# Hybrid HGRN2 and pooling block on one core: 8.25 products a half, pooled means in quarters, gates behind operands in the recurrent output projection

## The chip, the core and the metric

The kernel runs on one core of a Trainium2 chip, as one launch. Five engines with an instruction stream each take part: TensorE (PE), VectorE (DVE), ScalarE (ACT), GpSimd (POOL) and SyncE (SP), the last of which mainly issues DMA transfers; ScalarE and GpSimd issue a few too. The metric is the device time of a run in microseconds; the kernel before took 1466.38 us (median of 3 runs, 1464.82 to 1467.86).

## The reference

All tensors are float32, with 1024 tokens, width 1024, 8 heads of 128, and a hidden width of 4096. Cut to what matters:

```python
proj = x @ w_in                      # 7168 columns: q | f | i | og | pool_v | gate_a | gate_b
q = silu(q) * 128 ** -0.5
f = lb + (1 - lb) * sigmoid(f)       # lb from lb_logits, a softmax over two rows
# per head, in chunks: S_t = diag(f_t) S_{t-1} + (1 - f_t) i_t^T ;  o_t = S_t^T q_t
o = o * rsqrt(mean(o ** 2, per head) + 1e-6) * hgrn_norm_g * sigmoid(og)
a = o @ w_a
# trailing means over 2, 4, 8 and 16 tokens, one window to each quarter of the channels
b = per_group(mean_w(pool_v) - pool_v, w_pool) * pool_scale
mix = (sigmoid(gate_a) * a + sigmoid(gate_b) * b) @ w_out
x = LN(2 ** 0.25 * x + mix)
out = LN(2 ** 0.25 * x + relu(x @ w_up) ** 2 @ w_down)
```

## The kernel before

**Products.** Every large operand is split into a high part (a ScalarE cast to fp32r, L126 for weights and L131 for tokens) and a low part (a VectorE subtraction, L127 and L132). A product of two operands is three fp32r matmuls (high by high, high by low, low by high). The large products go by a two-by-two scheme with seven block products in place of eight: the 1024 tokens are two halves, the depth is two halves, and a `pair` takes two blocks of 128 weight columns. Its seven products are, with the operand on the weight side: `t0` for `p1`, `b_21` for `p2`, `t2` for `p6`, `t3` for `p7`, `t1` for `p5`, `t4` for `p4`, `b_22` for `p3` (with `twin` the middle four come as p7, p4, p6, p5). `t1` to `t4` are sums of weight blocks, made on VectorE in the tiles of the loaded blocks themselves (`make_t3` is L284). The token side has the operands `a11`, `a12`, `a22` and the sums `s1` to `s4`, resident in `xp`. One block product is `prod`: 12 matmuls of 128x128 by 128x512 into one PSUM bank (L212, L214, L215). Behind the products the quarters of the result are put together: `copied` (L275, ScalarE) empties a bank into a tile `c`, `added` (L279, VectorE) adds a second bank, and the function in `takes` does what the stage needs.

**Loads and rings.** Weight blocks of 512x128 (256 KB) come by SP's queue (`wide_block`, L223) into a ring of six tiles `raw`; `loaded_blocks` asks for blocks 11 and 21, one tile for the sum, then 12 and 22. Operand parts lie in a ring of ten tiles `w`. Results wait in a ring `c` of four plus two. A tile of a ring is given to its next use when the readers of its last use are done.

**Stages of the profiled execution.** To about 97 us: the value block `i` of the in-projection, with the tokens as the stationary side. `first_tokens` transposes x on TensorE (L170), `in_parts` splits it, `parts` splits rows of weights, `onto_chain` and `by_rows` multiply (`three`, from L501 on). In the source the calls of `parts(b11)` stand after `first_tokens("a11", ...)`; the ten short instructions for `lb`, `one_lb`, `e01` and `g_neg` (L440 to L449) stand ahead of both.

From 97 to 600 us: all other pairs of the in-projection up to gates 5, in the order of the list `ORDER`, and beside them the recurrence. The recurrence is a generator: `run` takes one turn of it after each block product (`next(turning[0], None)`). Half `n` is head n // 2, first or second 512 tokens. Its `prepare` pieces (VectorE, ScalarE, GpSimd), `turn_keys`, `scores`, `states`, `outputs` and `turn_outputs` are dealt over `PER_HALF` turns, in whole numbers by rounding a running sum (8.5: 8 and 9 alternating). The `inputs` pair of a head (q and f) must come before its half is prepared. `output_gates` and `gates` put sigmoids into DRAM (`og`, `ga`, `gb`). A `pooled` pair makes the trailing means in wide tiles `c` with a halo of 16 columns: `mean` works through two parts of 256 tokens with one to four additions each, and `put` stores the tile to `po`.

From 600 to 668.3 us: gates 6 and 7. Beside their 14 products goes the stream `pool_products`, by the counts of `POOL_AFTER` (how many of its steps follow each product), and what is left of the recurrence. A step multiplies a pooled operand by a block of `w_pool` (six matmuls, L113 to L115) and multiplies the result by a stored gate (`pb`). The weights of one group come by L618 into the single tile `tC`; their parts go round the four tiles `tD`, `tE`, `tF`, `og`. The tile `og` also holds the output gate of the half that is being finished (L1034), from which `put_output` stores the head, and with GpSimd's accumulating stores (L640) the sums `s1` to `s4` of the heads' outputs (`s` in the rows).

From 668.3 to some 780 us: the recurrent output projection `w_a` as four pairs with `turned` signs, the first two side by side. `o_operand` loads an operand of the heads' outputs (`o` in the rows, L618) and splits it, one name ahead of each product. `gated` loads a gate `ga` and a pooled result `pb`, multiplies (L1120) and adds; the first two pairs park their result. `room` is a ring of four tiles and `ga` one of twelve. Then come `w_out` and the first layer norm, the up projection with squared ReLU, and the down projection.

**Order.** From 97 to 668.3 us TensorE's order is the order of the program (`manual_schedule`). The order on the other engines, and on TensorE elsewhere, is chosen by the scheduler, by program order, `high_priority` and a model of times; `issue_after(i)` puts what is inside it behind instruction `i`. `behind_parts(name)` puts work behind the last two splits of a token operand.

The functions that the diff touches and those that call them:

Of the kernel before, what the change touches and what calls it, by code (L numbers as in the profile page):

```python
# [12 lines left out]
AF = mybir.ActivationFunctionType  # L13
# [16 lines left out]
PER_HALF = 8.5  # L30
# [21 lines left out]
def tile_hybrid_block(  # L52
# [105 lines left out]
    made_last, made_hi = {}, {}  # L158
# [108 lines left out]
    def pair(raw, rooms, takes, pz_tag="pj", twin=False, pc_tag="pj", turned=False):  # L267
# [35 lines left out]
        def t4():  # L303
            if twin:
                make_t2()
            if turned:
                minus_sum(b21, b11, b21)
            else:
                V.tensor_sub(b21, b21, b11)
            return w_part(b21)  # L310

        def t1():
            if turned:
                minus_sum(b12, b22, b11)
            else:
                V.tensor_sub(b12, b22, b11)
            return w_part(b12)
# [59 lines left out]
    turning = [iter(())]  # L377

    def run(*pairs, made=(), behind=()):

        for i, steps in enumerate(zip(*pairs)):
# [42 lines left out]
    with tc.tile_pool(name="xr", bufs=8, side="right", reuse_waits="tile") as xr:  # L424
# [15 lines left out]
        V.tensor_max(lb, prm[:, 0:8], prm[:, 8:16])  # L440
        V.tensor_sub(e01[:, 0:8], prm[:, 0:8], lb)
        V.tensor_sub(e01[:, 8:16], prm[:, 8:16], lb)
        A.activation(e01, e01, AF.Exp)
        V.tensor_add(lb, e01[:, 0:8], e01[:, 8:16])
        V.reciprocal(lb, lb)
        V.tensor_mul(lb, lb, e01[:, 0:8])
        V.tensor_scalar(one_lb, lb, -1.0, 1.0, ALU.mult, ALU.add)
        g_neg = e01[:, 0:8]
        V.tensor_scalar_mul(g_neg, g_col, -1.0)  # L449
# [109 lines left out]
        w = parts(b11)  # L559
# [60 lines left out]

    def o_operand(name):
# [23 lines left out]
    with tc.tile_pool(name="tmp", bufs=1, side="right", reuse_waits="tile") as tmp:  # L645
# [150 lines left out]
        def pooled(g):  # L796
# [3 lines left out]
            def mean(c, u):  # L800

                for lo in (QUARTER, 0):
                    pv = c[:, lo : lo + HALO + QUARTER]
                    cur = pv
                    for lev in range(g + 1):
                        s = 1 << lev
                        nx = small("pA" if lev % 2 == 0 else "pC", [P, HALO + QUARTER + HALO], 1)[:, : HALO + QUARTER]
# [722 lines left out]
```

## Time and profile before

| | before |
|---|---|
| median of 3 runs | 1466.38 us (1464.82 to 1467.86) |
| profiled execution, its time | 1466.59 us |
| its span | 1464.9 us |
| mean granted TensorE clock | 0.996 |
| DMA | 228.15 MB, mean 156 GB/s |
| L126 weight casts (ACT), 310 | 192.5 us |
| L127 weight splits (DVE), 310 | 212.1 us |
| L275 evictions (ACT), 96 | 55.8 us |
| L279 evictions (DVE), 95 | 64.8 us |

How the rows are read. A row of matmuls, casts or loads begins with its start in us from the start of the span and the mean duration of one; then engine, line, operation, out <- in, shapes and count; in brackets the idle time of the engine ahead of it and what ended that (`<-ACT c L275`: an instruction of ScalarE at line 275 that wrote a tile c). A row that begins with two times and a colon is a stretch of the span: its length, busy time of PE, of weight loads, DVE, ACT and POOL with counts, then the granted clock of TensorE, the mean share of the DMA engines in use, and GB/s. A row with `<-` between two instructions gives a kind of wait: total us, count, longest. SPq and POOLq are the sequencers that issue DMAs.

### The profile page before, as it was taken

Reading aid. Unit: us, or ns where it says so; the run is one execution under the profiler, and the core shown is the slowest. Engines: PE = TensorE matmul, PEld = TensorE weight load, DVE = VectorE, ACT = ScalarE, POOL = GpSimd, SP = SyncE. Lnnn points to the kernel's source line nnn. Section 1 sums busy time; section 2 is a strip of 40 time slices with the busy share of each in tenths; the row PEclk is TensorE's granted clock in tenths of the full one; section 3 lists DMA queues with packets and bytes.
Section 4 is the critical chain, followed back from the end, with each engine's and each line's share of the span. In section 5 each row is a group of like instructions: output and inputs, shape, how many; then the busy total and the mean of one; then the engine's idle time right before and its main releaser. Section 6 shows DMA issues by size and latency. Waiting matters only on the chain.

```text
span 1464.9 us, 20840 instructions
## 1 busy us (share of the span) xinstructions
PE 1435.5 (98%) x7377; PEld 1188.4 (81%) x7377; DVE 1100.1 (75%) x1807; ACT 759.0 (52%) x1383; POOL 107.6 (7%) x288
## 2 busy tenths in 40 slices
PE   8999999999999999999999999999999999999997
PEld 7788888788878888877788878888888888888886
DVE  4967886796797796477985598666666787777977
ACT  5545566655755655555542366555556443333435
POOL 0002011211211210000002100000000100000000
PEclk9999999999999999999999999999999999999999
DMA  7142245345435546788673135444447774445422
GB/s 259 58 137 87 73 126 169 80 134 155 109 87 146 142 116 184 211 300 286 204 232 113 61 99 180 144 154 148 157 148 261 280 262 142 166 132 170 129 72 115
DMA packets 187161, 228.15 MB, mean 156 GB/s; under 512 B 12176, under 2 KB 110512, under 8 KB 187056
## 3 DMA queue, kind: packets, MB, share of 16 engines
q1 hardware_dynamic: 181088, 212.91, 43.9%
q0 software_dynamic: 5184, 11.54, 4.0%
q10 hardware_dynamic: 784, 2.38, 0.5%
q8 instruction: 58, 0.95, 0.3%
q14 instruction: 47, 0.39, 0.1%
HBM read 149.70 MB, written 77.07 MB: 155 GB/s over the span
## 4 chain that ended last, share of the span: by engine, by line
PE 87%; DVE 6%; DMA 4%; issue 1%; ACT 1%; SPq 0%; DVEq 0%; POOL 0%; ACTq 0%
PE ps_pj L212 15%; PE ps_pj L215 14%; PE ps_pj L214 14%; PE ps_pj L1412 4%; PE ps_pj L1413 4%; PE ps_pj L1411 4%; PE ps_pj L114 2%; PE ps_pj L113 2%; PE ps_pj L115 2%; PE ps_tr L1412 1%; PE ps_tr L1413 1%; PE ps_tr L1411 1%; PE ps_sc L215 1%; DVE w L127 1%; PE ps_hg L215 1%
## 5 line engine op out<-in xcount | busy, mean ns | idle before, releaser
L212 PE MATMUL ps_pj<-act,w 128*128 128x512 f32 x1068 | 420.2, 395 | 10.8 <-ACT c L275 3.3
L215 PE MATMUL ps_pj<-act,w 128*128 128x512 f32 x1068 | 415.7, 391 | 1.3 <-DVE w L127 1.3
L214 PE MATMUL ps_pj<-act,w 128*128 128x512 f32 x1068 | 415.0, 390 | 0.0
L126 ACT CAST w<-raw 128x512 fp32r<-128x512 f32 x310 | 192.5, 622 | 278.1 <-PE ps_pj L214 201.7
L127 DVE TENSOR_TENSOR w<-raw,w 128x512 fp32r<-128x512 f32 x310 | 212.1, 686 | 92.8 <-ACT w L126 87.6
L212 PEld LDWEIGHTS ps_pj<-act,w 128*128 128x128 f32 x1068 | 200.7, 188 | 56.9 <-ACT c L275 4.6
L215 PEld LDWEIGHTS ps_pj<-act,w 128*128 128x128 f32 x1068 | 200.8, 188 | 45.2 <-DVE w L127 2.6
L214 PEld LDWEIGHTS ps_pj<-act,w 128*128 128x128 f32 x1068 | 200.8, 188 | 40.8 <-DVE act L132 0.2
L1373 ACT CAST act<-act 128x1024 fp32r<-128x1024 f32 x66 | 66.9, 1050 | 109.0 <-issue 35.0
L279 DVE TENSOR_TENSOR c<-c,ps_pj 128x512 f32<-128x512 f32 x95 | 64.8, 682 | 39.1 <-PE ps_pj L215 35.6
L1374 DVE TENSOR_TENSOR act<-act,act 128x1024 fp32r<-128x1024 f32 x66 | 79.5, 1220 | 18.5 <-ACT act L1373 17.4
L1413 PE MATMUL ps_pj<-act,act 128*128 128x512 f32 x240 | 93.0, 389 | 0.0
L1412 PE MATMUL ps_pj<-act,act 128*128 128x512 f32 x240 | 93.0, 389 | 0.0
L1411 PE MATMUL ps_pj<-act,act 128*128 128x512 f32 x240 | 92.5, 389 | 0.0
L275 ACT COPY c<-ps_pj 128x512 f32<-128x512 f32 x96 | 55.8, 581 | 3.1 <-issue 1.8
L284 DVE TENSOR_TENSOR raw<-raw,raw 128x512 f32<-128x512 f32 x43 | 29.6, 690 | 33.2 <-DMA raw<-in_w_in_dram 28.8
L1411 PEld LDWEIGHTS ps_pj<-act,act 128*128 128x128 f32 x240 | 45.0, 188 | 9.4
L1412 PEld LDWEIGHTS ps_pj<-act,act 128*128 128x128 f32 x240 | 45.0, 188 | 9.4
L1413 PEld LDWEIGHTS ps_pj<-act,act 128*128 128x128 f32 x240 | 45.0, 188 | 9.3
L1282 ACT ACTIVATE c<-c 128x512 f32<-128x512 f32 x61 | 38.5, 632 | 1.7
L1281 ACT ACTIVATE c<-c 128x512 f32<-128x512 f32 x46 | 29.1, 632 | 15.0 <-DVE c L279 15.0
L1367 DVE TENSOR_TENSOR act<-act,ps_pj 128x512 f32<-128x512 f32 x45 | 30.1, 682 | 6.0 <-PE ps_pj L1413 5.7
(416 smaller groups left out, 2680.5 us busy)
## 6 DMA issues: line engine op xcount, KB each, us to landing
h<-c SPq DMA_DIRECT2D x106, 256.0 KB, 2.7
raw<-in_w_in_dram SPq DMA_DIRECT2D x100, 256.0 KB, 3.3
act<-h SPq DMA_DIRECT2D x78, 256.0 KB, 3.0
draw<-in_w_down_dram SPq DMA_DIRECT2D x16, 1024.0 KB, 7.6
raw<-in_w_up_dram SPq DMA_DIRECT2D x56, 256.0 KB, 2.8
hf<-h SPq DMA_DIRECT2D x34, 256.0 KB, 3.0
s<-og POOLq DMA_DIRECT2D x28, 256.0 KB, 6.1
v<-v SPq DMA_DIRECT2D x16, 256.0 KB, 3.3
```

The lines of the kernel that those rows point to most:

```text
L126: A.copy(hi, src)
L127: V.tensor_sub(lo, src, f(hi))
L212: PE.matmul(ps, wh[:, k], th, start=first and k == 0, stop=False, skip_group_check=True)
L214: PE.matmul(ps, wh[:, k], tl, start=False, stop=False, skip_group_check=True)
L215: PE.matmul(ps, wl[:, k], th, start=False, stop=k == CH - 1, skip_group_check=True)
L275: A.copy(t, ps)
L279: V.tensor_add(t, t, ps)
L1373: A.copy(hi, src)
L1374: V.tensor_sub(lo, src, f(hi))
L1411: PE.matmul(ps, hh[:, w], wh, start=fresh and n == 0, stop=False, skip_group_check=True)
L1412: PE.matmul(ps, hh[:, w], wl, start=False, stop=False, skip_group_check=True)
L1413: PE.matmul(ps, hl[:, w], wh, start=False, stop=n == M - 1, skip_group_check=True)
```

## The change

Five edits. `PER_HALF` is 8.25 (8, 8, 8, 9 turns by rounding), inputs 7 precede gates 2, and the pool stream's steps beside gates 6 move towards the end by one product. In `pair`, `t2` is written into the tile of block 12 and `t1` into the tile of the difference, so block 11's tile is read last by `t2`. `mean` no longer works at once: it appends two entries to the list `later_on` (one for each part of 256 tokens, the second with the store), and `run` carries out one entry after each block product. At the start, weight rows 2 and 3 are split behind the token parts 1 and 3, and the lower-bound instructions behind all token parts. In `w_a`, the loads of `ga` and `pb` are put behind the last operand load issued, `room` has six tiles and serves all three results of a pair, and `ga` has ten.

```diff
-PER_HALF = 8.5
+PER_HALF = 8.25
@@ ORDER
-    ("gates", 2), ("inputs", 7), ("pooled", 3), ("gates", 3), ("gates", 4), ("gates", 5),
+    ("inputs", 7), ("gates", 2), ("pooled", 3), ("gates", 3), ("gates", 4), ("gates", 5),
-POOL_AFTER = {6: (1, 1, 1, 1, 1, 1, 2), 7: (2, 2, 2, 2, 0, 0, 0)}
+POOL_AFTER = {6: (0, 1, 1, 1, 1, 2, 2), 7: (2, 2, 2, 2, 0, 0, 0)}
@@ in_parts
-        made_last[name], made_hi[name] = (i.ins for i in split_into(xp[name][kp], src))
+        made_last[name], made_hi[name] = made_kp[name, kp] = [i.ins for i in split_into(xp[name][kp], src)]
@@ pair
-            return w_part(b11)
+            return w_part(b12)
         def make_t2():
             if turned:
-                minus_sum(b11, c["t"], b11)
+                minus_sum(b12, c["t"], b11)
             else:
-                V.tensor_add(b11, c["t"], b11)
+                V.tensor_add(b12, c["t"], b11)
         def t4():
...
-                V.tensor_sub(b21, b21, b11)
+                V.tensor_sub(b21, b21, b12)
         def t1():
...
-                V.tensor_sub(b12, b22, b11)
-            return w_part(b12)
+                V.tensor_sub(c["t"], b22, b12)
+            return w_part(c["t"])
@@ run
                     next(turning[0], None)
+                    if later_on:
+                        later_on.pop(0)()
@@ start: the ten lower-bound instructions leave L440 to L449
-        w = parts(b11)
+        w = parts(b11[:2])
+        for row, kp in zip(b11[2:], (1, 3)):
+            lo_done, hi_done = made_kp["a11", kp]
+            with tc.issue_after(lo_done), tc.issue_after(hi_done):
+                w += parts([row])
+        with behind_parts("a11"):
+            V.tensor_max(lb, prm[:, 0:8], prm[:, 8:16])
...
+            V.tensor_scalar_mul(g_neg, g_col, -1.0)
         first_tokens("a12", "tr")
@@ o_operand
-            split_into(xp[name][kp], loaded(src, c_tile))
+            t = c_tile()
+            last_load[0] = nc.sync.dma_start(out=t, in_=src).ins
+            split_into(xp[name][kp], t)
@@ pooled
-            def mean(c, u):
-                for lo in (QUARTER, 0):
-                    pv = c[:, lo : lo + HALO + QUARTER]
...
+            def mean(c, i, u):
+                later_on.append(lambda: quarter(c, u, QUARTER))
+                later_on.append(lambda: (quarter(c, u, 0), put(c, i, u)))
+            def quarter(c, u, lo):
+                pv = c[:, lo : lo + HALO + QUARTER]
...
             def first(c, i):
                 G.memset(c[:, :HALO], 0.0)
-                mean(c, 0)
-                put(c, i, 0)
+                mean(c, i, 0)
             def second(c, i):
-                mean(c, 1)
-                put(c, i, 1)
+                mean(c, i, 1)
@@ gated
             def take(src):
-                t = loaded(gad[j][u], mg_tile("ga", 12))
+                with tc.issue_after(last_load[0]):
+                    t = loaded(gad[j][u], mg_tile("ga", 10))
+                    more = loaded(pbd[j][u], mg_tile("gb", 2))
                 V.tensor_mul(t, t, src)
-                V.tensor_add(t, t, loaded(pbd[j][u], mg_tile("gb", 2)))
+                V.tensor_add(t, t, more)
@@ a_pair
-            room = mg_tile("room", 4)
+            room = mg_tile("room", 6)
-            return pair(raw, (c_tile, room, room), takes, "hg", True, turned=True)
+            return pair(raw, (room, room, room), takes, "hg", True, turned=True)
```

More of the change, by code (lines that the diff above doesn't have):

```diff
@@ L306, in t4 @@
             if turned:
[L307 removed]
+                minus_sum(b21, b12, b21)
             else:
[L309 removed]
+                V.tensor_sub(b21, b21, b12)
             return w_part(b21)
@@ L798, in pooled @@
             j, win = 2 * g, WINDOWS[g]
-            def mean(c, u):
-                for lo in (QUARTER, 0):
-                    pv = c[:, lo : lo + HALO + QUARTER]
[L804 to L807, printed above, removed]
-                        V.tensor_add(nx[:, 2 * s - 1 :], cur[:, 2 * s - 1 :], cur[:, s - 1 : HALO + QUARTER - s])
-                        cur = nx
-                    n = HALO
-                    if u == 0 and lo == 0:
-                        n += win - 1
-                        V.tensor_mul(cur[:, HALO:n], cur[:, HALO:n], inv_n[:, : win - 1])
-                        V.tensor_sub(pv[:, HALO:n], cur[:, HALO:n], pv[:, HALO:n])
-                    V.scalar_tensor_tensor(pv[:, n:], cur[:, n:], 1.0 / win, pv[:, n:], ALU.mult, ALU.subtract)
+            def mean(c, i, u):
[3 more added lines that the diff above has]
+                pv = c[:, lo : lo + HALO + QUARTER]
+                cur = pv
+                for lev in range(g + 1):
+                    s = 1 << lev
+                    nx = small("pA" if lev % 2 == 0 else "pC", [P, HALO + QUARTER + HALO], 1)[:, : HALO + QUARTER]
+                    V.tensor_add(nx[:, 2 * s - 1 :], cur[:, 2 * s - 1 :], cur[:, s - 1 : HALO + QUARTER - s])
+                    cur = nx
+                n = HALO
+                if u == 0 and lo == 0:
+                    n += win - 1
+                    V.tensor_mul(cur[:, HALO:n], cur[:, HALO:n], inv_n[:, : win - 1])
+                    V.tensor_sub(pv[:, HALO:n], cur[:, HALO:n], pv[:, HALO:n])
+                V.scalar_tensor_tensor(pv[:, n:], cur[:, n:], 1.0 / win, pv[:, n:], ALU.mult, ALU.subtract)
             def put(c, i, u):
```

25 lines of the change are left out of this document (12 added, 13 removed).

## The prediction, on record before the changed kernel ran

> **What bounds the kernel now.** I read the page's totals first, then the matmul waits with their times, then the stretches around each wait.
>
> ```profile
> span 1464.9 us, 20840 instructions
> PE 1435.5 (98%) x7377; PEld 1188.4 (81%) x7377; DVE 1100.1 (75%) x1807; ACT 759.0 (52%) x1383; POOL 107.6 (7%) x288
> 12.38:97.50 85.12, 84.36 (x384) 69.08 (x385) 67.86 (x115) 41.79 (x74) 0.76 (x7) 0.98 0.39 132
> 97.50:600.00 502.50, 496.50 (x3210) 415.65 (x3209) 392.63 (x794) 300.04 (x662) 83.36 (x236) 1.00 0.45 126
> 600.00:668.30 68.30, 64.83 (x274) 51.71 (x273) 46.52 (x73) 33.88 (x60) 2.62 (x3) 0.98 0.86 278
> 668.30:725.00 56.70, 53.19 (x230) 42.40 (x229) 48.03 (x78) 29.87 (x54) 0.00 (x0) 1.00 0.72 236
> 725.00:1464.90 739.90, 729.17 (x3245) 602.79 (x3243) 542.02 (x741) 349.10 (x530) 18.77 (x14) 1.00 0.47 159
> ```
>
> TensorE bounds it nearly everywhere. The rows give each stretch's length, then busy time of PE, weight loads, DVE, ACT, POOL, then the granted clock, DMA share and GB/s. The change moves no matmul out of the kernel, so it can win only PE's idle time before about 725 us and time at a reduced clock: 0.8 + 6.0 + 3.5 + 3.5 us in the four middle rows, and some at the start. Behind 725 us PE idles 10.7 us, nearly all at the end of the down projection, which the change leaves alone. The profiled execution took 1466.59 us, 1.7 us above its span; the median of the runs shown is 1466.38, so the two agree within 0.02%. About 0.2%, 2.9 us, is what a measurement of this kernel can tell from no change.
>
> **1. The start.** Two rows of windows, the first matmuls, and ScalarE ahead of them:
>
> ```profile
> 12.00:14.00 2.00, 1.62 (x5) 1.34 (x6) 2.00 (x6) 2.00 (x5) 0.00 (x0) 0.77 1.06 400
> 14.00:16.00 2.00, 2.00 (x6) 1.54 (x6) 1.52 (x6) 2.00 (x5) 0.00 (x0) 0.50 1.04 384
> 16.00:18.00 2.00, 2.00 (x10) 1.60 (x9) 1.18 (x2) 0.77 (x2) 0.00 (x0) 0.87 1.06 388
> 9.27 0.66 PE L170 MATMUL ps_sc<-ident,x 128*128 128x128 f32 x4 [1.28 <-DMA x<-in_x_dram]
> 9.76 0.60 PE L170 MATMUL ps_hg<-ident,x 128*128 128x128 f32 x4
> 12.38 0.50 PE L501 MATMUL ps_pj<-w,act 128*128 128x512 f32 x1 [2.02 <-ACT act L131]
> 7.87 0.62 ACT L126 CAST w<-b 128x512 fp32r<-128x512 f32 x1 [1.82 <-DMA b<-in_w_in_dram]
> 10.60 1.14 ACT L126 CAST w<-b 128x512 fp32r<-128x512 f32 x2 [2.12 <-DMA b<-in_w_in_dram]
> 11.76 1.05 ACT L131 CAST act<-ps_tr 128x512 fp32r<-128x512 f32 x2
> ```
>
> The token casts (L131) stand behind the casts of weight rows 2 and 3, which arrive at 10.6 us, though the transposes of the first two token tiles were done when PE fell idle, at 9.27 - 1.28 = 7.99. The change puts rows 2 and 3, and the ten lower-bound instructions, behind the token parts. ScalarE is free at 8.49 us, so two token casts of 0.5 us each end by about 9.6, before the last transposes end at 10.36: the 2.02 us go. Rows 2 and 3 are late next: cast from about 11.2 us, split by VectorE by 14.5, and needed only when the 24 matmuls of the first two weight rows (12 each, 729.17/3245 = 0.22 us a matmul by the last stretch) have gone by: 10.4 + 24 x 0.22 = 15.7. The clock was granted at 0.77, 0.50 and 0.87 in the three windows, a loss of 0.46 + 1.00 + 0.26 = 1.7 us, right behind that idle time. With the gap gone I take the loss as gone too: -3.7 us. Lower bound of the gain 0 (VectorE absorbs it later, below), upper 3.7.
>
> The Trainium skill (TensorE: Matmul & The Clock Gate, "Part 1: The HAM clock gate") says an idle activity window halves the clock and a busy one of about 3.4 us restores it; the three rows agree in depth and length. It also says the window runs freely, so the cold stretch varies from run to run, which speaks against booking it; by that the start is worth 2.0 us and the forecast would stand 1.7 us higher.
>
> **2. The recurrence.** The five waits of 0.88, 1.62, 0.74, 1.47 and 1.29 us make the 6.0:
>
> ```profile
> 263.59 0.50 PE L212 MATMUL ps_pj<-act,w 128*128 128x512 f32 x1 [0.88 <-ACT c L275]
> 289.36 0.50 PE L212 MATMUL ps_pj<-act,w 128*128 128x512 f32 x1 [1.62 <-ACT c L275]
> 319.77 0.50 PE L212 MATMUL ps_pj<-act,w 128*128 128x512 f32 x1 [0.74 <-DVE f L279]
> 433.32 0.50 PE L212 MATMUL ps_pj<-act,w 128*128 128x512 f32 x1 [1.47 <-ACT f L275]
> 437.62 0.50 PE L212 MATMUL ps_pj<-act,w 128*128 128x512 f32 x1 [1.29 <-DVE f L279]
> 120.00:590.00 470.00, 464.00 (x3058) 388.47 (x3057) 376.78 (x770) 281.00 (x623) 83.36 (x236) 1.00 0.45 125
> 420.00:450.00 30.00, 27.24 (x184) 22.36 (x183) 26.44 (x59) 18.89 (x40) 6.66 (x16) 1.00 0.43 109
> 510.00:540.00 30.00, 30.00 (x205) 25.21 (x203) 28.65 (x64) 16.45 (x40) 4.39 (x12) 1.00 0.46 130
> DVE raw L284 <- DMA raw<-in_w_in_dram: 28.8, 16, 4.5
> SPq L223 <- DVE w L127: 127.7, 43, 9.7
> ```
>
> All five are late evictions: VectorE is at 376.78/470 = 24.0 of 30 us, and in crowded windows PE waits. At 8.25 products a half, 17 halves have 140.25 products instead of 144.5: the same VectorE work in 3.0% less room, at most 24.8 of 30. Against it, the pooled quarters come one behind each product: no instruction more, but a burst of up to four quarters is spread over four products, and its four stores land up to four products later; the tiles they hold are asked for again only by the second pair after, so no wait follows. Yet the fullest window, 510 to 540 (the widest pooled pair), lost nothing, so spreading is not where the six are.
>
> T2 written into b12 and T1 into the difference's tile leaves the count of instructions. The second load of a pair can start two products earlier. The fourth, for whose arrival L284 waited 28.8 us in all, still waits for the split (L127) of the sixth product's operand, and T1 is now made one product before it is used instead of four. So I book 0: the waits change places. Bounds: -6.0 if all go, +5 if the 3% adds two windows like 420:450 (2.76 each). Inputs 7 ahead of gates 2 moves seven products and their four loads without a new one: 0.
>
> **3. Pool products beside gates 6 and 7.**
>
> ```profile
> 608.97 0.74 DVE L1034 SCALAR_TENSOR_TENSOR og<-ps_tr,e,og 128x512 f32<-128x512 f32 x1
> 610.00 2.62 POOL L640 DMA_DIRECT2D s<-og  x3 [25.82 <-DVE og L1034]
> 620.52 0.69 DVE L127 TENSOR_TENSOR og<-tC,tF 128x512 fp32r<-128x512 f32 x1 [2.31 <-DMA s<-og]
> 622.30 0.67 SPq L618 DMA_DIRECT2D tC<-in_w_pool_dram  x1
> 627.71 0.62 ACT L126 CAST tD<-tC 128x512 fp32r<-128x512 f32 x1 [3.37 <-DMA tC<-in_w_pool_dram]
> 628.90 0.50 PE L212 MATMUL ps_pj<-act,w 128*128 128x512 f32 x1 [2.16 <-ACT w L126]
> 630.30 0.50 PE L215 MATMUL ps_pj<-act,w 128*128 128x512 f32 x1 [0.67 <-DVE w L127]
> 632.00:634.00 2.00, 2.00 (x6) 1.52 (x6) 0.11 (x1) 0.00 (x0) 0.00 (x0) 0.50 1.08 344
> ```
>
> One chain: the last head's gain (L1034), its accumulating stores, the low half of the pool weights into the same tile (2.31 us late), the load of the next pool weights behind it, ScalarE stuck 3.37 us on that load with the operand of gates 6's last product queued behind, PE idle 2.16 + 0.67, and then 3.4 us at half clock, 1.7 us. Together 4.5. The recurrence ends four products earlier; in the instruction order of the changed kernel the split into og precedes the fourth product's operand of gates 6 instead of the sixth's, while ScalarE's cast of the next pool weights keeps its place before the seventh. The 14 products of gates 6 and 7 fill the stretch of 68.3 us, 4.9 us each with what goes beside them, so the load has two products, 9.8 us, more, against 3.37 needed: -4.5. In return L1034 and that split now have products with fewer pool steps between them; the store took 620.52 - 609.71 = 10.8 us, and VectorE can wait 2.31 + 1.4 us (one pool step of six matmuls less, 6 x 0.22) with operands queued behind. Bounds 0 to 3.7; I take 1.5, nearer to the old wait, which cost PE nothing. Net -3.0.
>
> **4. w_a.**
>
> ```profile
> 677.39 5.89 SPq L618 DMA_DIRECT2D ga<-ga  x4
> 683.69 0.32 SPq L618 DMA_DIRECT2D c<-o  x1
> 688.59 1.14 ACT L131 CAST act<-c 128x512 fp32r<-128x512 f32 x2 [3.36 <-DMA c<-o]
> 689.26 0.49 PE L212 MATMUL ps_hg<-act,w 128*128 128x512 f32 x1 [2.13 <-ACT act L131]
> 699.71 0.50 PE L212 MATMUL ps_pj<-act,w 128*128 128x512 f32 x1 [0.99 <-ACT room L275]
> 656.49 1.68 SPq L223 DMA_DIRECT2D raw<-in_w_a_dram  x3
> ```
>
> SP's queue was held 5.9 us by four gate loads; the operand behind them (683.69) came late: 2.13 us. In the new order all 28 operand loads precede the first gate load, so that goes, and six rooms instead of four take the 0.99. What comes: the gate products (L1120) stand behind the last operand splits on VectorE, and eight gate loads, three weight blocks and four pooled loads follow in a row. 15 x 256 KB at 236 GB/s are 16.7 us for some 17 us of VectorE work; a wait of 0 to 3 us, I take 1.0. Two weight blocks now queue behind operands of s2 that wait for gates 7's fourth product: gates 7's last three products of 12 matmuls and the two pool steps beside its fourth end that stretch, so the fourth ends near 668.3 - 3 x 2.7 - 2.7 = 657.5; with the split behind it the blocks are issued near 660 instead of 656.5. The second pair uses them from 668.3 + 2.7 = 671, and a load took 688.59 - 683.69 = 4.9 us: covered, by some 6 us. Net -2.1.
>
> The Trainium skill (DMA: Bandwidth & Descriptors, "Issuing engines are not separate DMA queues") has all issuers share the same 16 DMA engines; the stretches of 0.86 and 0.72 DMA share agree. By it reordering makes no bandwidth, and this part would be worth 0, the total 2.1 us more.
>
> Nothing else in the up and down projections gains or loses: T2 and T1 are made on VectorE there too, at 542 of 740 us busy.
>
> **Sum.** -3.7 + 0 - 3.0 - 2.1 = -8.8: span 1456.1, time 1457.8 us.
>
> **Rivals.**
> - Only the start: parts 2 to 4 exchange one wait for another (28.8 us of L284 and 10.8 us of store speak for it). 1466.6 - 3.7 = 1462.9.
> - It doesn't do what it says: VectorE is 67.86 of 85.12 us busy behind the start, and absorbs the lead, while 3 and 4 exchange waits: 1466.6. Against: VectorE's backlog begins with a wait for the transposes, which move along.
> - Slower: VectorE becomes the bound of the recurrence. If every second of the 16 halves has a window like 420:450, that is 8 x 2.76 = 22.1 in place of 6.0, +16.1, net +7.3: 1473.9. It ends above 1469.5 from (8.8 + 6.0 + 2.9)/2.76 = 6.4 such windows on. For it: the 3%; against it: 28.65 of 30 cost nothing at 510.
>
> **Chances.** The sum 0.50, only the start 0.18, no effect 0.12, VectorE bound 0.20. Faster takes the first and two thirds of the second, 0.62; same a third of the second and most of the third, 0.16; slower 0.22. The first case's own range is 1451 to 1463 (6.0 more won in part 2; or 5 lost there). To leave out 2 in 10 the whole reaches from 1451 to 1470.
>
> **What would show it.** Part 1: no wait of 2 us before the first L501, clock 1.00 from 12 to 18 us. Part 2: PE idle about 6 us from 97 to 600. Part 3: no ScalarE wait on tC, no reduced clock near 630; a DVE wait on s<-og instead. Part 4: no c<-o wait on ScalarE beside ga loads. Wrong if PE idles over 9 us in the recurrence, or a new wait of over 2 us with a halved clock appears around w_a.

## The result, and the profile after

The changed kernel takes 1462.19 us (median of 20 runs, 1457.27 to 1466.81), the kernel before 1466.12 in as many: a ratio of 0.9972, 95% interval 0.9962 to 0.9983. That is 3.9 us faster by the medians and 4.1 by the ratio, where 8.6 were forecast. The direction was right, half the gain is missing. The profiled execution took 1464.25 us, 2.1 above the median, with a span of 1462.6. One execution of a run below, c_gate_late, took 2054.45 us at a mean granted clock of 0.654, and is in no ratio.

The changed kernel's totals and stretches, cut where its own stages begin (columns as before: length, then busy time of PE, weight loads, DVE, ACT, POOL, then clock, DMA share, GB/s):

```profile
span 1462.6 us, 20884 instructions
PE 1435.4 (98%) x7377; PEld 1190.3 (81%) x7377; DVE 1100.2 (75%) x1807; ACT 759.2 (52%) x1383; POOL 106.7 (7%) x288
12.38:92.98 80.60, 80.12 (x376) 66.02 (x375) 65.89 (x114) 40.03 (x72) 0.76 (x7) 1.00 0.42 144
92.98:603.31 510.33, 501.68 (x3218) 418.93 (x3216) 393.97 (x796) 302.71 (x664) 85.11 (x239) 0.99 0.45 125
603.31:672.65 69.34, 63.32 (x266) 50.35 (x264) 48.73 (x78) 36.69 (x67) 0.00 (x0) 0.98 0.87 291
672.65:729.50 56.85, 56.85 (x252) 47.10 (x251) 49.63 (x81) 27.82 (x50) 0.00 (x0) 1.00 0.66 219
729.50:1462.60 733.10, 723.45 (x3222) 598.76 (x3221) 537.39 (x732) 345.94 (x523) 18.78 (x14) 1.00 0.46 159
```

The kernel before, cut at the same two stages (recurrence, pool products):

```profile
97.50:600.89 503.39, 497.39 (x3214) 416.38 (x3212) 393.21 (x795) 300.91 (x663) 83.36 (x236) 1.00 0.45 126
600.89:668.17 67.28, 63.81 (x270) 50.84 (x268) 45.94 (x73) 32.91 (x58) 2.62 (x3) 0.97 0.86 278
```

Stage by stage: the value block ends 4.5 us earlier (97.50 to 92.98). The recurrence is 6.9 us longer: TensorE's idle time is up from 6.0 to 8.65 us, and behind two of its waits the clock is lower (0.51 on average from 505.5 to 509 us, 0.57 from 566.5 to 570.5), which loses 1.7 us each time. The pool products are 2.1 us longer, idle time from 3.5 to 6.0. From w_a to the end the rest is 6.8 us shorter (796.7 to 790.0): w_a's stretch has no idle time at all. The idle time of the rest fell by 4.6 us (3.5 + 10.7 to 9.65); what the other 2.2 us are is not known. The sum is -2.3, the difference of the spans.

TensorE's long waits in the changed kernel, with the start's first product on top and two windows of the start below:

```profile
10.05 0.48 PE L493 MATMUL ps_pj<-w,act 128*128 128x512 f32 x1
310.05 0.50 PE L212 MATMUL ps_pj<-act,w 128*128 128x512 f32 x1 [1.04 <-ACT f L275]
449.18 0.50 PE L212 MATMUL ps_pj<-act,w 128*128 128x512 f32 x1 [2.18 <-ACT c L275]
505.64 0.80 PE L212 MATMUL ps_pj<-act,w 128*128 128x512 f32 x1 [2.25 <-DVE c L279]
565.42 0.50 PE L212 MATMUL ps_pj<-act,w 128*128 128x512 f32 x1 [2.08 <-ACT c L275]
645.46 0.80 PE L212 MATMUL ps_pj<-act,w 128*128 128x512 f32 x1 [4.96 <-ACT w L126]
12.00:14.00 2.00, 2.00 (x10) 1.67 (x9) 1.32 (x4) 2.00 (x5) 0.00 (x0) 1.00 1.05 405
14.00:16.00 2.00, 2.00 (x10) 1.67 (x9) 0.82 (x3) 1.17 (x3) 0.00 (x0) 1.00 1.05 386
```

The start is as forecast: the first product at 10.05 instead of 12.38 us, no wait, full clock. The five short late evictions of before are gone; one of 1.04 us and three of over 2 us stand elsewhere. A wait of 4.96 us in gates 7 is new.

### The profile page after: what moved, and what is told of

Same layout as the page of the kernel before. It is cut to its first block, busy times and chain, and to the rows that moved or that the text cites. A ratio compares the mean times of both kernels' runs of the same rounds, so it can differ in the third digit from the quotient of the medians.

```text
span 1462.6 us, 20884 instructions
## 1 busy us (share of the span) xinstructions
PE 1435.4 (98%) x7377; PEld 1190.3 (81%) x7377; DVE 1100.2 (75%) x1807; ACT 759.2 (52%) x1383; POOL 106.7 (7%) x288
## 4 chain that ended last, share of the span: by engine, by line
PE 85%; DVE 7%; DMA 4%; issue 2%; ACT 1%; SPq 0%; DVEq 0%; POOL 0%; ACTq 0%; POOLq 0%
PE ps_pj L212 14%; PE ps_pj L215 14%; PE ps_pj L214 14%; PE ps_pj L1425 4%; PE ps_pj L1426 4%; PE ps_pj L1427 4%; PE ps_pj L114 2%; PE ps_pj L113 2%; PE ps_pj L115 2%; PE ps_tr L1425 1%; PE ps_tr L1426 1%; PE ps_tr L1427 1%; PE ps_hg L215 1%; PE ps_hg L214 1%; PE ps_sc L215 1%
## 5 line engine op out<-in xcount | busy, mean ns | idle before, releaser
L215 PE MATMUL ps_pj<-act,w 128*128 128x512 f32 x1068 | 417.1, 391 | 0.6 <-DVE w L127 0.4
L126 ACT CAST w<-raw 128x512 fp32r<-128x512 f32 x311 | 192.9, 622 | 273.9 <-PE ps_pj L214 186.1
L127 DVE TENSOR_TENSOR w<-raw,w 128x512 fp32r<-128x512 f32 x311 | 213.0, 687 | 103.1 <-ACT w L126 101.8
L215 PEld LDWEIGHTS ps_pj<-act,w 128*128 128x128 f32 x1068 | 201.6, 189 | 44.6 <-DVE w L127 1.7
L284 DVE TENSOR_TENSOR raw<-raw,raw 128x512 f32<-128x512 f32 x43 | 29.6, 689 | 31.3 <-DMA raw<-in_w_in_dram 29.2
```

Source lines behind the costliest of these rows:

```text
L126: A.copy(hi, src)
L127: V.tensor_sub(lo, src, f(hi))
L215: PE.matmul(ps, wl[:, k], th, start=False, stop=k == CH - 1, skip_group_check=True)
```

## Experiments

All times are medians beside runs of the kernel before on the same chip; the ratio is to those. "c" stands for the changed kernel with the old counts: 8.5 products a half, the old order and the old pool counts. Line numbers are those of each run's own kernel: in the changed one the loads of L618 are L625, the accumulating stores of L640 are L651 and the gain of L1034 is L1046; in the runs with w_a's first operand late, L126, L127 and L215 are L128, L129 and L217, and L793 is L799.

| run | edit | us | ratio (95%) |
|---|---|---|---|
| after | the change | 1462.2 | 0.9972 (0.9962, 0.9983) |
| b_start | before + start | 1461.5 | 0.9970 (0.9960, 0.9981) |
| b_wa | before + w_a | 1460.0 | 0.9967 (0.9954, 0.9979) |
| b_both | before + start + w_a | 1457.4 | 0.9941 (0.9927, 0.9954) |
| a_old_count | c itself | 1453.8 | 0.9921 (0.9909, 0.9934) |
| c_new_order | c, inputs 7 first | 1455.5 | 0.9933 (0.9920, 0.9946) |
| c_mean_at_once | c, means at once | 1457.2 | 0.9931 (0.9915, 0.9946) |
| c_old_tiles | c, old operand tiles | 1457.0 | 0.9940 (0.9927, 0.9953) |
| a_old_pool | after, old pool counts | 1464.4 | 0.9991 (0.9978, 1.0003) |
| a_gate_late | after, gate load later | 1462.1 | 0.9969 (0.9958, 0.9980) |
| c_gate_late | c, gate load later | 1455.3 | 0.9926 (0.9912, 0.9939) |
| a_far_pool | after, one product on GpSimd | 1466.4 | 0.9998 (0.9987, 1.0009) |
| a_no_means | after, no means | 1452.3 | 0.9906 (0.9892, 0.9919) |
| a_no_accum | after, no accumulating stores | 1453.8 | 0.9913 (0.9901, 0.9926) |
| a_a11_late | after, w_a's first operand late | 1462.0 | 0.9969 (0.9956, 0.9982) |
| c_a11_late | c, w_a's first operand late | 1452.0 | 0.9903 (0.9888, 0.9918) |
| c_v_a11 | c_a11_late, pool weights not in og | 1466.0 | 0.9998 (0.9988, 1.0008) |
| c_np_a11 | c_a11_late, new pool counts | 1451.2 | 0.9882 (0.9866, 0.9899) |
| c_sp_a11 | c_a11_late, spread counts | 1452.2 | 0.9894 (0.9879, 0.9909) |

**Which part gains and which costs.** The start's hunks alone, w_a's hunks alone (`o_operand`, `gated`, `a_pair`), and both, on the kernel before:

> The kernel before with the start's edit alone (rows 2 and 3 behind token parts, lower-bound instructions behind all parts). Theory 1: the first product of inputs 0 begins 4 to 4.5 us earlier and nothing later gives it back: 4 us faster, 1462. Rival: VectorE or the loads of the stages behind absorb the lead: within 1 us of the kernel before.

> The kernel before with w_a's edit alone (loads of ga and pb behind the last operand load, six rooms). Theory 1: the waits of 2.13, 0.99, 0.29 and 0.25 us in w_a go, and no new one comes: 3.5 to 4.5 us faster, 1462. Rival: the DMA engines bound w_a, the order of the loads makes no difference: within 1 us. Forecast on record: 2.1 us faster.

> The kernel before with the start's and w_a's edits alone, old operand tiles, pooled means at once. If the parts add (start 4.2, w_a 5.6 less what the profile's spread makes): 1456 to 1458. The new operand tiles and the quarters, which the run with the old count has besides (1453.8), are then worth 2 to 4 us; the rival is that they are worth nothing: 1453 to 1455.

The start with its clock (first row, of b_start), and w_a (second row, of b_wa):

```profile
0.00:97.00 97.00, 93.80 (x442) 78.30 (x443) 71.46 (x123) 47.31 (x82) 2.82 (x35) 1.00 0.47 161
```

```profile
668.00:760.00 92.00, 91.59 (x404) 75.55 (x403) 76.97 (x124) 43.63 (x78) 0.00 (x0) 1.00 0.66 213
```

0.30% and 0.33% faster alone, 0.59% together: the two parts add, and make more than the whole change does (0.28%). So another part must cost. The count was undone, with all the rest left as changed:

```diff
-PER_HALF = 8.25
+PER_HALF = 8.5
-    ("inputs", 7), ("gates", 2), ("pooled", 3),
+    ("gates", 2), ("inputs", 7), ("pooled", 3),
-POOL_AFTER = {6: (0, 1, 1, 1, 1, 2, 2),
+POOL_AFTER = {6: (1, 1, 1, 1, 1, 1, 2),
```

> The changed kernel with 8.5 products a half, the old order (gates 2 before inputs 7) and the old pool counts. Start, operand tiles of a pair, quarters and w_a stay as changed. Theory 1: the 3% less room in the recurrence costs what the profile shows, some 6.5 us more excess between 97 and 600 us (three waits of 2.1 to 2.3 us with a lower clock behind two of them): without it about 1456 to 1458, and TensorE's idle time from 97 to 600 us at 6 us or less. Rival: quarters or the new operand tiles crowd VectorE, not the count: 1461 to 1464, idle time there stays over 8 us.

1453.8 us: 8.4 less than the changed kernel, 7.5 by the ratios. The three lines together cost that much; more than the forecast's sum of all gains is there without them. In the profiles all of it lies in the recurrence, cut as above where it and gates 6 begin: 500.57 us here, 510.33 as changed, while the pool products are no shorter (70.31 and 69.34). This is no accident of one execution: the other runs with 8.25 that leave VectorE's work and the stores alone (a_old_pool, a_gate_late, a_a11_late) have 510.5 to 510.8 us there, all runs with 8.5 on the changed kernel 500.4 to 502.7. Then one part of it, or one further part of the change, was put back or taken out. `c_new_order` has the first and third line of that diff alone, `a_old_pool` the third alone; `c_mean_at_once` calls both parts and `put` from `mean`; `c_old_tiles` has `pair` as before.

> 8.5 products a half and the old pool counts, but inputs 7 ahead of gates 2; all other edits as changed. Theory 1 (the count costs, since eight turns a half leave no turn without VectorE work): the order of the two pairs is innocent, 1453 to 1456, idle time of TensorE from 97 to 600 us within 2 us of the run with the old count. Rival (the swap crowds the stretch from 440 to 510 us, where two of the three long waits of the changed kernel lie): 1457 to 1460, with waits of about 2 us there.

> 8.5 products a half, old order and old pool counts; start, operand tiles and w_a as changed, but a pooled tile's two parts made at once and not one behind each product. Theory 1: quarters are worth at most 1 to 2 us (the waits at 433 and 437 us of the kernel before lie behind pooled 2 and went with them): 1454 to 1456. Rival: quarters carry the gain in the recurrence: 1457 or more.

> 8.5 products a half, old order and old pool counts; start, quarters and w_a as changed, but t2 written into block 11's tile and t1 into block 12's as before. Theory 1: the new tiles are worth 1 to 2 us in the recurrence, since the second load of a pair starts two products earlier (the waits of the split sum for a weight load fell from 28.8 to 23.9 us): 1454 to 1456. Forecast on record: nothing, 1454. Rival: they carry most of it: 1457 or more.

> The changed kernel with the old counts of pool steps, (1,1,1,1,1,1,2) beside gates 6. Theory 1: the new wait of 4.96 us in gates 7 comes from six products in a row with two pool steps each, which the four tiles f cannot serve (loads of gates and stores of results queue on SP, and the operand loads of w_a behind them). With one product fewer at two steps it shrinks to under 1.5 us and the lower clock behind it goes: about 5 us under the changed kernel, near 1457. Rival: the wait is there because the cast of a w_a operand stands ahead of a gate operand's cast on ScalarE, whatever the counts: 1461 to 1463, and a wait of 4 to 5 us remains in gates 7. Second rival: the old wait on the tile og comes back (2.2 us near the end of gates 6): 1459.

The order of the two pairs costs little, if anything: 0.12% by the ratios (1.8 us) with intervals that overlap by half, and the recurrence takes 502.53 us with it. Quarters and tiles are worth some 1.5 and 2.8 us by the ratios, both together 2.9 (b_both against a_old_count), with intervals that overlap; neither is settled as to its size. With old tiles a wait of the kernel before (437.62) is back in its place:

```profile
432.39 0.50 PE L212 MATMUL ps_pj<-act,w 128*128 128x512 f32 x1 [1.28 <-DVE f L279]
```

The pool counts are not the cost either: with the old ones at 8.25 the kernel is no faster (0.9991 against 0.9972, intervals that overlap a little). That leaves the 8.25, and c_new_order and a_old_pool differ in nothing else: 0.9933 against 0.9991, 8.5 us, with intervals far apart, and 502.53 against 510.80 us in the recurrence. In its pool stage a_old_pool shows the split into og waiting for the last head's stores, then SP's queue held by a gate load with a weight block behind it, and TensorE idle:

```profile
610.94 0.69 DVE L127 TENSOR_TENSOR og<-tC,tF 128x512 fp32r<-128x512 f32 x1 [5.46 <-DMA s<-og]
627.11 0.32 SPq L625 DMA_DIRECT2D f<-gb  x1
627.49 0.43 SPq L223 DMA_DIRECT2D raw<-in_w_in_dram  x1
633.30 0.49 PE L212 MATMUL ps_pj<-act,w 128*128 128x512 f32 x1 [2.79 <-DVE raw L301]
```

**Why the recurrence loses.** Of the changed kernel, how the wait at 505 us comes about: GpSimd issues three accumulating stores, SP a weight block; the DMA engines' share of that stretch and the packets of the two kinds of queue from 480 to 498 us (packets, MB, share of 16 engines); VectorE from the late block to the eviction that TensorE waits for; the clock behind it.

```profile
483.51 2.66 POOL L651 DMA_DIRECT2D s<-og  x3 [6.15 <-DVE og L1046]
484.10 0.38 SPq L223 DMA_DIRECT2D raw<-in_w_in_dram  x1
484.00:492.50 8.50, 8.50 (x40) 6.99 (x39) 1.86 (x5) 1.73 (x3) 2.29 (x4) 1.00 1.02 209
q0 software_dynamic: 432, 0.79, 30.4%
q1 hardware_dynamic: 1550, 1.34, 24.0%
493.91 0.69 DVE L284 TENSOR_TENSOR raw<-raw,raw 128x512 f32<-128x512 f32 x1 [6.90 <-DMA raw<-in_w_in_dram]
499.47 1.27 DVE L900 TENSOR_TENSOR_SCAN tA<-starts,f 128x256 f32<-128x256 f32 x2
504.91 0.67 DVE L279 TENSOR_TENSOR c<-c,ps_pj 128x512 f32<-128x512 f32 x1
504.00:506.00 2.00, 0.36 (x1) 0.36 (x2) 2.00 (x6) 1.98 (x7) 0.42 (x3) 0.88 0.38 129
506.00:508.00 2.00, 2.00 (x6) 1.52 (x6) 2.00 (x5) 1.99 (x4) 0.00 (x0) 0.50 0.01 2
508.00:510.00 2.00, 2.00 (x8) 1.62 (x7) 1.97 (x4) 0.86 (x3) 0.00 (x0) 0.76 0.35 131
```

The block is issued at 484.10 and used at 493.91, while the stores fill the DMA engines. VectorE stands 6.90 us, then works off the recurrence's pieces without a pause from 499.47, and the eviction (504.91) comes behind them. The lower clock loses 0.24 + 1.00 + 0.48 = 1.7 us more. Three causes were conceivable: SP's queue, VectorE's room, the late blocks. Each was taken on by itself.

SP: the load of the output gate two turns later. It leads SP's queue and waits there for the stores out of the same tile.

```diff
-                self.og = loaded(ogd[self.h][self.u], lambda: tt("og"))      # in outputs
+                    if turn == TURN_BACK - 2 and old:
+                        old.load_gate()                                      # the same load
```

> The changed kernel (8.25) with the load of a head's output gate (tile og, a ring of one) asked for two turns later, two turns before it is used. Theory 2: at 8.25 SP waits 58.4 us in 13 waits (longest 9.2) for the stores of the previous half out of that tile, with the weight blocks of the pairs queued behind it; a late block makes VectorE late and then the evictions. Asked for later, SP waits under 25 us there, the long waits of 2.1 to 2.3 us in the recurrence go, and the time falls by 4 to 7 us to 1456 to 1458. Rival (the room on VectorE and ScalarE is short, whatever SP does): SP's wait falls, the three waits stay: 1461 to 1463. It can be slower if the gate then lands too late for its product.

> 8.5 products a half, old order, old pool counts, all else as changed, and the output gate's load two turns later as above. Theory 2: SP waits 47.5 us there with 8.5 products too, and the three waits left (1.30, 1.22 and 1.25 us) lie behind it: 2 to 4 us faster than with the old counts alone, 1450 to 1452. Rival: 1453 to 1455.

Neither moved. The wait itself did not shrink, as the sequencer's waits show (total us, times, longest), so the run takes nothing away and says little on its theory. After first, then a_gate_late:

```profile
SPq L625 <- DMA s<-og: 58.4, 13, 9.2
```

```profile
SPq L625 <- DMA s<-og: 60.6, 12, 8.9
```

VectorE's room: `far_queries` on GpSimd (`G.tensor_mul` in place of `V.tensor_mul`), and a kernel that leaves the work of the means out (`quarter` returns at once; the pooled branch then carries the values themselves).

> The changed kernel (8.25) with one VectorE product of each half (far_queries, some 0.68 us) made on GpSimd. If VectorE's room is what is short at 8.25 (0.25 products or about 0.8 us a half, of which VectorE is busy four fifths), the three waits of 2.1 to 2.3 us in the recurrence shrink by half or more: 1456 to 1459. If not VectorE but the rhythm (which instructions of a half stand ahead of an eviction) makes them, they stay: 1461 to 1463.

> The changed kernel without the work on the pooled means: the quarters keep their place and their store, but add nothing, so VectorE has some 40 us less to do in four stretches. If VectorE's room were what is short, the wait of 2.18 us at 449 us (beside the means of pooled 2) goes, and those at 505 and 565 us too if they are a backlog from there: 4 us or more faster, 1458 or less. If the output gate's load on SP's queue makes them (theory 2), at least two of the three stay: 1460 to 1463.

The late blocks: the 28 accumulating stores left out, so the sums of the heads' outputs lack terms.

> The changed kernel without the accumulating stores of the heads' outputs into the sums (28 stores by GpSimd left out, so the sums lack terms). Theory 3: at 8.25 VectorE has too little room to catch up after a weight block that comes late, and the latest (6.90 us at 494 us) is late because three accumulating stores saturate the DMA engines from 484 to 492 us beside it. Without them that wait of VectorE falls under 3 us, the wait of TensorE at 505 us (2.25) goes, the wait of SP on s<-og goes everywhere; those at 449 and 565 us, whose late pieces are others, stay within 1 us: 2 to 5 us faster than the changed kernel, 1457 to 1460. If room on VectorE alone decides, all three stay: 1461 to 1463. If the accumulating stores make all of them: 1455 or less.

The recurrence, cut as above, of a_old_count, a_far_pool, a_no_means and a_no_accum, each followed by VectorE's wait for late blocks from 97 to 600 us; for a_far_pool instead the product on GpSimd and a product of VectorE that falls beside it:

```profile
92.65:593.22 500.57, 496.74 (x3214) 416.58 (x3212) 392.48 (x794) 301.65 (x663) 81.51 (x236) 1.00 0.45 127
DVE raw L284 <- DMA raw<-in_w_in_dram: 23.9, 16, 2.6
```

```profile
92.86:608.73 515.87, 504.04 (x3217) 419.83 (x3216) 396.21 (x780) 302.15 (x664) 105.00 (x255) 0.99 0.45 124
L998 POOL TENSOR_TENSOR tA<-q,eq 128x512 f32<-128x512 f32 x16 | 19.8, 1239 | 15.4 <-DVE q L949 15.4
L957 DVE TENSOR_TENSOR q<-q,p 128x128 f32<-128x128 f32 x16 | 11.8, 738 | 0.0
```

```profile
92.74:591.25 498.51, 497.01 (x3217) 417.00 (x3216) 355.63 (x668) 302.08 (x664) 86.44 (x239) 1.00 0.46 128
DVE raw L284 <- DMA raw<-in_w_in_dram: 29.4, 16, 4.6
```

```profile
92.63:594.20 501.57, 497.94 (x3217) 416.75 (x3216) 394.62 (x797) 302.94 (x664) 60.02 (x211) 1.00 0.37 115
DVE raw L284 <- DMA raw<-in_w_in_dram: 20.4, 15, 3.1
```

TensorE's idle time there is 3.8 us with the old count, 1.5 without the means and 3.6 without the accumulating stores, against 8.65 as changed. Without the means the blocks are as late in sum (29.4 us, 28.1 as changed), the latest by 4.6 us in place of 6.9, and VectorE makes it good. Without the accumulating stores VectorE has all its work, the latest block comes 3.1 us late, and the recurrence takes what it takes with 8.5; the waits at 449 and 565 us, which that run's expectation kept, shrank too (to 1.46 and 0.90). Taking away either is enough. The reading is that it takes both: blocks made late by accumulating stores, and too little room on VectorE to catch up. Of the two the stores are the better shown, since without the means the latest block is less late too. SP's queue is not parted from them altogether: without the stores its waits on L625 fall from 58.4 to 12.4 us as well. But without the means they are 63.2 us and TensorE hardly waits, and the block behind the wait at 505 us was not held in the queue; it was issued at 484.10, right behind the transfer before it, and landed 9.7 us later. What leads to the waits at 449 and 565 us was not followed piece by piece. Both runs also gain in other stages, so their whole times are not the price of the recurrence alone.

a_far_pool says nothing on VectorE's room, because it gave VectorE none. `far_queries` takes 1.24 us on GpSimd instead of 0.68, and VectorE's instruction beside it ends only when GpSimd's has ended (one of L957 runs from 225.17 to 226.30 us beside 225.06 to 226.16): L957 takes 0.74 us on average in place of 0.28 and L944 0.59 in place of 0.41. VectorE has 16 instructions less, and its busy time in the whole kernel rose from 1100.2 to 1102.1 us. TensorE's idle time rose to 11.8 us; why so far is open.

Open too: with the old count the latest block is 2.6 us late, although the same stores are made. That they fall beside other loads there is likely, but not shown. So the count may cost by where it puts the stores as much as by the room that it takes.

**Why the pool stage loses.** In the changed kernel ScalarE stands 7.20 us at the cast of a loaded head output (L131), for w_a's first operand, and the operand of gates 7 is queued behind it; the load was issued at 639.56:

```profile
639.56 0.47 SPq L637 DMA_DIRECT2D c<-o  x1
644.27 0.62 ACT L131 CAST act<-c 128x512 fp32r<-128x512 f32 x1 [7.20 <-DMA c<-o]
644.80 0.61 ACT L126 CAST w<-raw 128x512 fp32r<-128x512 f32 x1
```

`o_operand("a11")` was put behind the split for gates 7's fifth product, with the new and with the old counts:

```diff
-        o_operand("a11")
+        with tc.issue_after(gate_splits[0]), tc.issue_after(gate_splits[1]):
+            o_operand("a11")
```

> The changed kernel (8.25, new pool counts) with w_a's first operand loaded and split only behind the split for gates 7's fifth product. Theory: the wait of 4.96 us at 645 us is ScalarE's stand of 7.20 us at the cast of a loaded head output ahead of a gate operand's cast; behind the fifth product it and the lower clock go: 4 to 6 us faster than the changed kernel, 1456 to 1458. Rival (the gates' ring f and the loads of the pool stage bound it at two steps a product): a wait of over 2 us stays in gates 7, 1460 or more.

> 8.5 products a half, old order, old pool counts, all else as changed; w_a's first operand is loaded and split only behind the split for gates 7's fifth product. In the pool stage TensorE waits 2.63 us because ScalarE stands 4.84 us at the cast of a loaded head output with a gate operand's cast behind it. Theory: that wait and the lower clock behind it go, 3 to 4 us faster than with the old counts alone, 1450 to 1451. Rival: the loads of the pool stage are the bound (DMA share 1.0 there), or the first product of w_a now waits for its operand: 1453 or more.

With 8.25 a wait of 3.01 us for a pool step whose gate came late took the place of the 4.96 (a_a11_late), as the rival has it. In the profiles the stage is 3.3 us shorter even so (66.06 us), but the whole kernel shows nothing of it (1462.0 and 1462.2 us). With the old count it went, and one for og stayed (c_a11_late); the gain over a_old_count is 0.18%, with intervals that overlap.

```profile
644.78 0.75 DVE L799 SCALAR_TENSOR_TENSOR f<-ps_tr,prm,f 128x512 f32<-128x512 f32 x1 [4.11 <-DMA f<-gb]
645.59 0.69 PE L113 MATMUL ps_tr<-w,tD 128*128 128x512 f32 x1 [3.01 <-DVE f L799]
```

```profile
613.78 0.69 DVE L129 TENSOR_TENSOR og<-tC,tF 128x512 fp32r<-128x512 f32 x1 [2.59 <-DMA s<-og]
615.12 0.50 PE L217 MATMUL ps_pj<-act,w 128*128 128x512 f32 x1 [2.61 <-DVE w L129]
```

Against that last wait three things were tried: the weights' parts in the tiles v (`ring("tD", "tE", "v", "v")`, the held results in tF and og), the changed kernel's pool counts, and counts of (1, 1, 1, 1, 1, 1, 1) and (2, 2, 2, 2, 1, 0, 0).

> 8.5 products a half, old order and pool counts, w_a's first operand late as above, and the parts of the pool weights in tD, tE and the two tiles v instead of tD, tE, tF and og. The last long wait of the pool stage (2.61 us and a lower clock behind it) follows the split into og, which stands 2.59 us for the last head's stores. Theory: it goes, 3 to 4 us faster than 1452, 1448 to 1449.5. Rival: the chain's next member (gate ring f, DMA share 1.0) takes its place: 1451 to 1453.

> 8.5 products a half, old order, w_a's first operand late, and the changed kernel's pool counts (no step behind gates 6's first product). The one wait left in the pool stage with the old counts, 2.61 us for the split into og that stands for the last head's stores, gets one more product of cover (4.9 us): it goes, 1448 to 1450. Rival (two steps a product for six products in a row are more than the gates' ring and the DMA engines give, as at 8.25): a wait of 2 us or more in gates 7 takes its place, 1452 to 1455.

> The same with the pool steps spread as thin as their use allows, (1,1,1,1,1,1,1) and (2,2,2,2,1,0,0): four products in a row with two steps in place of five. If the rate of steps is the pool stage's bound, no wait for a gate in gates 7; the wait for og (2.61 us) stays: 1451 to 1453. If w_a's first product then waits for work moved next to it: 1454 or more.

With v the wait for og is gone; instead TensorE waits 3.05 us for a late weight block at 623.68, and w_a's first product 7.99 us (first row, c_v_a11). With the new counts the split waits longer than before (3.90 us), yet TensorE loses 0.97 us behind it in place of 2.61 (c_np_a11); presumably it now stands ahead of a later product's operand, one product being worth 4.9 us:

```profile
679.23 0.79 PE L214 MATMUL ps_pj<-act,w 128*128 128x512 f32 x1 [7.99 <-ACT w L128]
```

```profile
613.58 0.69 DVE L129 TENSOR_TENSOR og<-tC,tF 128x512 fp32r<-128x512 f32 x1 [3.90 <-DMA s<-og]
616.79 0.50 PE L217 MATMUL ps_pj<-act,w 128*128 128x512 f32 x1 [0.97 <-DVE w L129]
```

The spread counts keep the wait for og, as expected. c_np_a11, at 0.9882, is the fastest of all; it beats the changed kernel by 0.9%, and c_a11_late and c_sp_a11 by less than the intervals tell.

## Why the prediction was half right

**1, the start: right, a little low.** Forecast -3.7, in the profile -4.5, alone 0.30%. The lead is kept to the end, and the lower clock right behind the gap went with it (1.00 in the two windows above). The sentence drawn from the Trainium skill (TensorE: Matmul & The Clock Gate, "Part 1: The HAM clock gate"), by which that 1.7 us should not be booked, would have been the worse choice here: of the 18 profiled executions with the start's edit one lost the 1.7 us even so (c_mean_at_once, clock 0.61 and 0.54 from 10 to 14 us, behind a wait of 1.60 us for x).

**2, the recurrence: the step that failed.** "So I book 0: the waits change places. Bounds: -6.0 if all go, +5 if the 3% adds two windows like 420:450 (2.76 each)." The waits did change places, but into three long ones, +6.9 us by the profile, 1.9 beyond the bound; the count alone costs 8.3 there (502.53 to 510.80). Three errors sit in it. A lower clock behind such waits was put at nothing, and it makes 3.4 of the 6.9; so the sign set for this part, over 9 us of idle time, did not show (8.65). The 3% was spread evenly, 24.8 of 30 us, though a half of nine turns has one turn without a piece of `prepare` and one of eight has none; 8.25 has four halves of nine turns where 8.5 has eight. That these free turns decide, and not the mean, is argued from the program; no run took them away by themselves. And the wait of L284 for late blocks (28.8 us in all) was read as hidden, because TensorE had not paid for it; it was paid for by VectorE's room, and where three accumulating stores made a block 6.90 us late, the room did not suffice. The rival "VectorE becomes the bound" named the right engine and asked for eight windows; there were three.

**3, the pool products: the wait went, and its successor was not foreseen.** Forecast -3.0, measured +2.1 by the profile. TensorE's wait of 2.16 and 0.67 us on tC's chain is gone. VectorE's wait for og grew from 2.31 to 5.79 us, past the 3.7 that bounded it, and cost TensorE nothing; the forecast had priced it at 1.5:

```profile
610.47 0.69 DVE L127 TENSOR_TENSOR og<-tC,tF 128x512 fp32r<-128x512 f32 x1 [5.79 <-DMA s<-og]
```

What costs is ScalarE's wait at w_a's operand, with TensorE's 4.96 us behind it. The forecast named the reverse risk, w_a's blocks behind those operands, and not that a cast for w_a stands ahead of a cast for gates 7. With the operand late and the recurrence at 8.5 the new counts leave no wait over 1.2 us (c_np_a11), though not by the forecast's way, an earlier end of the recurrence.

**4, w_a: right, low.** Forecast -2.1, a gain of 3.1 less 1.0 for a new wait. The stretch went from 3.5 us idle to none, no new wait came. The ten gate loads now stand in one row of SP's queue behind the operands. Alone it is 0.33%, 4.8 us. By what the Trainium skill states (DMA: Bandwidth & Descriptors, "Issuing engines are not separate DMA queues"), that all issuers share the same 16 DMA engines, the prediction's rival took this part to be worth 0. No run here speaks against the sharing, but the 0 did not follow from it: with the same traffic, the order in one queue was worth 4.8 us. "Nothing else gains" missed a little: behind 725 us the idle time fell from 10.7 to 9.65 us, in the up projection.

```profile
682.65 5.16 SPq L625 DMA_DIRECT2D ga<-ga  x10
```

By the profile the four parts missed by -0.8, +6.9, +5.1 and, with all behind the pool products, -4.7 us. That the total is only half off, and in the right direction, is in part luck: w_a gained more than forecast and hid part of what the recurrence and the pool products lost. The recurrence, the one part where a schedule was tightened, was priced at its mean load.

## What to carry to other kernels

A schedule that interleaves two streams can be bounded by its recovery and not by its mean load, as this one seems to be: look for the turns that carry nothing before taking them out. A wait of an engine off the critical path is free only as long as that engine has room behind it. A wait that brings the lower clock with it costs more than its length, here 1.7 us more each time. When several edits come as one, run each alone and each undone: here all but one gave 0.79%, and all of them 0.28%.

## What the runs showed of the hardware

Accumulating stores are dear: from 480 to 498 us they moved 0.79 MB in 30.4% of the DMA engines' time, all other transfers 1.34 MB in 24.0%, twice the engine time for a byte, and a 256 KB load beside them took 9.7 us to land instead of a median of 3.2. The queue by itself is not what makes them so: from 1140 to 1170 us plain loads of GpSimd in the same queue, 512 KB each, moved 4.10 MB in 37.1% of the engines' time, 43 us of one engine for a MB where the stores took 111.

A product moved to GpSimd can cost VectorE as much as it saves: the 16 products that a_far_pool moved had taken 10.9 us there, and VectorE's busy time was no lower without them, since what it did beside them became slower.

Waits of about 2 us can halve the clock, and need not. Behind 2.25 us at 505 and 2.08 at 565 it fell to 0.50; behind 2.18 us at 449, in the same kernel, it did not (rows below), though in a_gate_late it did behind 1.79 us at that place (0.70 and 0.50 from 450 to 454 us).

```profile
449.00:451.00 2.00, 1.82 (x8) 1.52 (x9) 1.92 (x5) 2.00 (x7) 0.00 (x0) 1.00 0.11 29
451.00:453.00 2.00, 2.00 (x11) 1.65 (x10) 1.97 (x5) 1.12 (x3) 0.21 (x2) 1.00 0.35 107
```

The Trainium skill (TensorE: Matmul & The Clock Gate, "Part 1: The HAM clock gate") has a free-running window of about 3.4 us decide. That equal waits differ agrees with a window that runs on by itself; that a wait of 1.79 us, about half the stated window, can be enough is what the measurement adds. It may be one reason why runs of the changed kernel lie 9.5 us apart.
